# Casting all weight pieces before the next x, and multiplying before transposing, in a batched matmul on one core

## The chip, the cores and the metric

The kernel runs on one core of one Trainium2 chip. The metric is the time of one execution on the device, in microseconds; a smaller time is better. Each of the core's engines runs its own queue of instructions in order: TensorE (PE) multiplies and transposes, VectorE (DVE) and ScalarE (ACT) copy and convert, SyncE (SP) issues the transfers, GpSimd (POOL) only builds an identity matrix at the start. They wait for one another through counting semaphores. Sixteen transfer (DMA) engines move data between the device's memory (HBM) and the on-chip buffers.

## The reference

128 independent products of a 256x512 matrix with a 512x384 matrix, all in float32:

```python
b1, b2, m, k, n = 8, 16, 256, 512, 384
x = randn(b1, b2, m, k); weight = randn(b1, b2, k, n)
out = np.matmul(x, weight)
```

## The kernel before

**Groups.** Four batch items form a group (`G = 4`), so there are `NG = 32` groups, numbered 0 to 31. For each group SP loads x (2048 KB) and the weights (3072 KB) as float32 and stores the result (1536 KB). x and weights have two buffers each in float32 (`XS`, `WS`), the results four (`OS`).

**What each engine does for a group.**

- VectorE converts x to bf16 in four pieces (`cast_x`, line 171; one piece is two of a partition's eight rows). There is one bf16 buffer for x (`BS = 1`), so piece q of a group waits until TensorE has transposed piece q of the group before (`t_made`).
- The weights are converted to bf16 in sixteen pieces of 32 partitions x 1536 elements (`cast_w`, line 184): the first `CV` by VectorE, the last `CA` by ScalarE, with `CV + CA = 16`. Before the change these are 11 and 5. The bf16 weights have room for two groups (`WBS = 2 * G`), so casting a group waits for the multiplication of the group before the last (`p_made`). In groups 0 to 3, 30 and 31 (`is_short`) VectorE converts all weights in eight pieces of 64 partitions (`cast_short`, line 200) and ScalarE only counts its semaphore up.
- TensorE transposes x in four quarters of four instructions each (`transpose`, line 224) into PSUM (`pt`, four buffers); ScalarE copies each quarter to the on-chip buffer `x_t` (`evacuate`, line 211).
- TensorE multiplies in four quarters of 32 instructions (`multiply`, line 242), each on a 32-column strip of the array; the last group has another layout (`multiply_full`, line 260). A multiplication first waits for all sixteen weight pieces of its group (`w_acast`, `w_vcast`), then, quarter by quarter, for the copied transposes (`t_copied`) and for a free result buffer (`o_copied`; `po` has two).
- ScalarE copies each quarter's result out of PSUM (`copy_out`, line 275).

**The order on SP** (`on_sync`). For each group m from 4 on: load x of m (after `x_cast` of group m-2), store the result of group m-4 (after its `copy_out`), load the weights of m (after both engines' casts of group m-2). Each of these waits holds up what is behind it on SP.

**The order on VectorE** (`on_vector`, `step`). For group n: eight weight pieces (`XV = 8`), then the four pieces of x of group n+1, then the other three weight pieces of n.

**The order on TensorE** (`on_tensor`). Transposes of group n+1, then the multiplication of group n; the loop handles two groups per turn.

**The order on ScalarE** (`on_scalar`, `step`). For group n: copy three quarters of the transposes of n+1, copy out the first quarter of n, copy the last quarter of the transposes, then copy out the other quarters of n; after the second and the third copy-out one weight piece each of group n+1, and after the fourth the remaining three.

Of the kernel before, what the change touches and what calls it, by code (L numbers as in the profile page):

```python
# [12 lines left out]
def kernel(  # L13
# [30 lines left out]
    T = R // 2  # L44
# [6 lines left out]

    LAG = 4

    CA = 5
    CV = G * SL - CA
    HV = G * SH

    XV = 8

    PAD = 12  # L60

# [58 lines left out]
    def is_short(n):  # L120
        return isinstance(n, int) and (n < LAG or n >= NG - 2)
# [4 lines left out]
    def load_w(e, t, U, s):  # L126
        n = t * U + s
        if not isinstance(n, int) or n >= WS:
            e.wait_ge(w_vcast, n * CV + (1 - WS) * CV)
            e.wait_ge(w_acast, n * CA + (1 - WS) * CA)  # L130
        d = SL // SH if is_short(n) else 1
# [32 lines left out]
    def cast_x(e, t, U, s, q):  # L164
        n = t * U + s
        if q == 0:
            e.wait_ge(x_in[s % XS], (t * (U // XS) + s // XS) * 16 + 16)
        e.wait_ge(t_made, n * T + (q + 1 - T + BIAS))  # L168
        rows = slice(2 * q, 2 * q + 2)
        S = SH if is_short(n) else SL  # L170
        e.tensor_copy(  # L171
            out=x_bf[s % BS][:, rows].rearrange("p r (s q c) -> p r s q c", s=S, c=KO),
            in_=x_sb[s % XS][:, rows].rearrange("p r (q s c) -> p r s q c", s=S, c=KO),
        ).then_inc(x_cast, 1)

    def cast_w(e, t, U, s, parts, first=True):
        n = t * U + s
        if first:
            e.wait_ge(p_made, n * T + (BIAS - T))
            e.wait_ge(w_in[s % WS], (t * (U // WS) + (s - LAG) // WS) * 16 + 16)  # L180
        copy = e.tensor_copy if e is nc.vector else e.copy
        for c in parts:
            i, h = c // SL, c % SL
            copy(  # L184
                out=w_bf[(s * G + i) % WBS][h * C : (h + 1) * C],
                in_=w_sb[s % WS][i * C : (i + 1) * C, h * KO : (h + 1) * KO, :],
            ).then_inc(w_vcast if c < CV else w_acast, 1)

    def cast_short(e, n):
        e.wait_ge(p_made, n * T + (BIAS - T))  # L190
        p = P // SH
        for d in range(SL // SH):
            turns = n // WS if n < LAG else LAG // WS
            e.wait_ge(h_in[n % WS * 2 + d], turns * 16 + 16)  # L194
            for a in range(SH):
                for h in range(SH):
                    c = d * 4 + a * 2 + h
                    r = (d * SH + h) * KO

                    e.tensor_copy(  # L200
                        out=w_bf[(n * G + d * SH + a) % WBS][h * p : (h + 1) * p],
                        in_=w_sb[n % WS][a * p : (a + 1) * p, r : r + KO, :],
                    ).then_inc(w_vcast, 2 if c < CV - HV else 1)

    def evacuate(e, t, U, s, parts=range(T)):
        n = t * U + s
        if parts[0] == 0:
            e.wait_ge(p_made, n * T + (BIAS - T))
        for q in parts:
            e.wait_ge(t_made, n * T + (q + 1 + BIAS))  # L210
            e.copy(  # L211
                out=x_t[s % TS][:, 2 * q : 2 * q + 2],
                in_=pt[(s * T + q) % PT][:].bitcast(bf16),
            ).then_inc(t_copied, 1)

    def transpose(e, t, U, s):
        n = t * U + s
        words = x_bf[s % BS][:].bitcast(fp32)
        for q in range(T):
            e.wait_ge(x_cast, n * T + (q + 1))  # L220
            e.wait_ge(t_copied, n * T + (q + 1 - PT + BIAS))
            for rr in range(2):
                for h in range(KO // 2):
                    ins = e.transpose(  # L224
                        pt[(s * T + q) % PT][:, rr, h, :],
                        words[:, 2 * q + rr, h :: KO // 2],
                        identity[:],
                    )
            ins.then_inc(t_made, 1)

    def multiply(e, t, U, s):
        n = t * U + s
        e.wait_ge(w_acast, n * CA + CA)
        e.wait_ge(w_vcast, n * CV + CV)
        for q in range(T):
            e.wait_ge(t_copied, n * T + (q + 1 + BIAS))
            e.wait_ge(o_copied, n * T + (q + 1 - PO + BIAS))
            for rr in range(2):
                for ko in range(KO):
                    for i in range(G):  # L240
                        mine = slice(i * C, (i + 1) * C)
                        ins = e.matmul(  # L242
                            po[(s * T + q) % PO][mine, rr, :N],
                            x_t[s % TS][:, 2 * q + rr, ko // 2, mine, ko % 2],
                            w_bf[(s * G + i) % WBS][:, ko, :],
                            start=(ko == 0),
                            stop=(ko == KO - 1),
                        )
            ins.then_inc(p_made, 1)

    def multiply_full(e, t, U, s):
        n = t * U + s
        e.wait_ge(w_acast, n * CA + CA)
        e.wait_ge(w_vcast, n * CV + CV)
# [14 lines left out]
    def copy_out(e, t, U, s, q):  # L269
        n = t * U + s  # L270
        if q == 0:
            if not isinstance(n, int) or n >= OS:
                e.wait_ge(o_out[s % 2], (t * (U // 2) + s // 2) * 16 + (16 - OS // 2 * 16 + 16))
        e.wait_ge(p_made, n * T + (q + 1 + BIAS))
        e.copy(  # L275
            out=out_sb[:, bass.ds(slot(t, U, s) * R + 2 * q, 2), :],
            in_=po[(s * T + q) % PO][:, :, :N],
        ).then_inc(o_copied, 1)
# [33 lines left out]
    def on_vector(e):  # L312
        U = 2

        def next_x(t, U, s):
            for q in range(T):
                cast_x(e, t, U, s + 1, q)

        def step(t, U, s):
            n = t * U + s  # L320
            if is_short(n):
                cast_short(e, n)
            else:
                cast_w(e, t, U, s, range(XV))
            if not isinstance(n, int) or n < NG - 1:
                next_x(t, U, s)
            if not is_short(n):
                cast_w(e, t, U, s, range(XV, CV), False)

        next_x(0, NG, -1)  # L330
        for n in range(LAG):
            step(0, NG, n)
        rounds = (NG - 3 - LAG) // U
        with e.Fori(0, rounds) as t:  # L334
            for s in range(U):
                step(t, U, LAG + s)
        for n in range(LAG + rounds * U, NG):
            step(0, NG, n)

    def on_tensor(e):  # L340
        U = 2
        e.sem_inc(t_made, BIAS)
        e.sem_inc(p_made, BIAS)
        e.wait_ge(id_done, 2)
        transpose(e, 0, NG, 0)

        pe = mybir.EngineType.PE
        with nc.Fori(0, NG // U, engines=OrderedEngineSet([pe]), head_slot={pe: 0}) as t:
            transpose(e, t, U, 1)
            multiply(e, t, U, 0)  # L350
            with e.If(t < NG // U - 1):
                transpose(e, t, U, 2)
                multiply(e, t, U, 1)
            with e.Else():
                multiply_full(e, t, U, 1)

    def on_scalar(e):
        U = 2
        e.sem_inc(t_copied, BIAS)
        e.sem_inc(o_copied, BIAS)  # L360
        for s in range(2):
            e.sem_inc(o_out[s], 16)

        def step(t, U, s):
            short = is_short(t * U + s + 1)
            evacuate(e, t, U, s + 1, range(T - 1))
            for q in range(T):
                copy_out(e, t, U, s, q)  # L370
                if q == 0:
                    evacuate(e, t, U, s + 1, range(T - 1, T))
                if q == 0 and short:
                    e.sem_inc(w_acast, CA)
                if q > 0 and not short:
                    last = CA if q == T - 1 else q
                    cast_w(e, t, U, s + 1, range(CV + q - 1, CV + last), q == 1)

        evacuate(e, 0, NG, 0)
        e.sem_inc(w_acast, CA)  # L380
        for n in range(LAG - 1):
            step(0, NG, n)
        rounds = (NG - 2 - LAG) // U
        with e.Fori(0, rounds) as t:
            for s in range(LAG - 1, LAG - 1 + U):
                step(t, U, s)
        for n in range(LAG - 1 + rounds * U, NG - 1):
            step(0, NG, n)
        for q in range(T):
            copy_out(e, 0, NG, NG - 1, q)  # L390

    on_gpsimd(nc.gpsimd)
    on_sync(nc.sync)
    on_vector(nc.vector)
    on_tensor(nc.tensor)
    on_scalar(nc.scalar)

# [29 lines left out]
```

## Time and profile before

| | |
|---|---|
| time, median of 3 runs (lowest to highest) | 517.62 us (517.43 to 517.68) |
| profiled execution | 517.57 us, its span 515.8 us |
| TensorE: matmul busy, mean granted clock | 320.0 us (62%), 0.778 of full |
| VectorE busy | 397.7 us (77%) |
| ScalarE busy | 409.7 us (79%) |
| transfers' share of the 16 engines' span | 99.3%, 218.11 MB, mean 423 GB/s |
| VectorE weight cast, 32x1536 (line 184) | x286, mean 951 ns |
| ScalarE weight cast, 32x1536 (line 184) | x130, mean 1470 ns |
| VectorE x cast (line 171) | x128, mean 688 ns |
| ScalarE copy of transposes (line 211) | x128, mean 1021 ns |
| ScalarE copy-out (line 275) | x128, mean 800 ns |
| 3072 KB of weights, issue to landing (median) | 18.2 us |
| 2048 KB of x, issue to landing (median) | 22.3 us |
| 1536 KB of result, issue to landing (median) | 25.0 us |

The span runs from the first to the last instruction of the profiled execution. Busy times are sums of instruction durations; where instructions overlap in an engine's pipeline, the distance from one start to the next can be shorter than a duration. The times to landing contain the time that a transfer stands behind others. The granted clock is the share of its full speed that TensorE's clock has at a time.

### The profile page before, as it was taken

What the parts mean: (1) busy time and instruction counts of PE and PEld (TensorE: products, weight loads), DVE (VectorE), ACT (ScalarE), POOL (GpSimd) and SP (SyncE); (2) the same over time, 40 slices, a digit from 0 to 9 for tenths busy, and PEclk for the clock granted to TensorE, in tenths of its full rate; (3) what the DMA queues carried; (4) which work ended last, traced back from release to release, by engine and by line L of the source; (5) the groups of instructions that cost most, each with busy time, mean ns of one, the idle gap of its engine ahead of it and who ended that gap; (6) DMA issues with size and microseconds to landing.
All of it is one profiled execution on the core that took longest, in us unless ns stands there. A gap on an engine that the chain in (4) does not pass through costs nothing.

```text
span 515.8 us, 11659 instructions
## 1 busy us (share of the span) xinstructions
PE 320.0 (62%) x4512; PEld 222.0 (43%) x4512; DVE 397.7 (77%) x462; ACT 409.7 (79%) x387; POOL 0.7 (0%) x6
## 2 busy tenths in 40 slices
PE   2276737567586656675655864767657477656871
PEld 2254425444354443453443543535445354434550
DVE  2788757788777897777977778877789777797960
ACT  1365577798978997987998799889798978997751
POOL 0000000000000000000000000000000000000000
PEclk9698878677866877876888686778667876877697
DMA  8999999999999999999999999999999999999996
GB/s 337 428 423 426 437 430 420 435 431 433 431 424 432 430 439 428 429 426 432 433 436 428 423 434 431 437 429 425 430 431 434 433 429 427 430 435 423 421 429 250
DMA packets 15462, 218.18 MB, mean 423 GB/s; under 512 B 1632, under 2 KB 1632, under 8 KB 2656
## 3 DMA queue, kind: packets, MB, share of 16 engines
q1 hardware_dynamic: 15456, 218.11, 99.3%
q8 instruction: 3, 0.05, 0.0%
q14 instruction: 3, 0.02, 0.0%
HBM read 167.77 MB, written 50.33 MB: 423 GB/s over the span
## 4 chain that ended last, share of the span: by engine, by line
DMA 57%; DVE 29%; issue 9%; PE 1%; DVEq 1%; SPq 1%; ACT 0%; POOLq 0%
DMA w_sb<-in_weight_dram 57%; DVE w_bf L184 20%; DVE x_bf L171 5%; DVE w_bf L200 4%; PE po L260 1%; SPq L135 0%; DVEq L334 0%; SPq L118 0%; DVEq L62 0%; DVEq L180 0%; ACT out_sb L275 0%; SPq L130 0%; DVEq L168 0%; DVEq L194 0%; SPq L422 0%
## 5 line engine op out<-in xcount | busy, mean ns | idle before, releaser
L184 DVE CAST w_bf<-w_sb 32x1536 bf16<-32x1536 f32 x286 | 271.9, 951 | 81.1 <-DMA w_sb<-in_weight_dram 73.0
L242 PE MATMUL po<-w_bf,x_t 128*32 128x384 bf16 x3968 | 201.5, 364 | 33.4 <-DVE w_bf L184 25.4
L224 PE MATMUL pt<-identity,x_bf 128*128 128x128 f32 x512 | 113.5, 409 | 149.1 <-DVE x_bf L171 149.1
L184 ACT CAST w_bf<-w_sb 32x1536 bf16<-32x1536 f32 x130 | 191.0, 1470 | 5.1 <-DMA w_sb<-in_weight_dram 1.9
L224 PEld LDWEIGHTS pt<-identity,x_bf 128*128 128x128 f32 x512 | 101.3, 223 | 161.5 <-issue 161.0
L242 PEld LDWEIGHTS po<-w_bf,x_t 128*32 128x32 bf16 x3968 | 117.7, 107 | 116.3 <-issue 51.5
L275 ACT COPY out_sb<-po 128x768 f32 (+1 forms) x128 | 102.5, 800 | 59.7 <-PE po L242 53.9
L211 ACT COPY x_t<-pt 128x1024 bf16<-128x1024 bf16 x128 | 123.6, 1021 | 20.9 <-PE pt L224 20.3
L171 DVE CAST x_bf<-x_sb 128x1024 bf16<-128x1024 f32 x128 | 80.0, 688 | 12.5 <-DMA x_sb<-in_x_dram 11.7
L200 DVE CAST w_bf<-w_sb 64x1536 bf16<-64x1536 f32 x48 | 45.8, 955 | 8.3 <-DMA w_sb<-in_weight_dram 7.0
L211 ACT ACT_TABLE_LOAD x1 | 1.3, 1283 | 10.8 <-PE pt L224 10.8
L260 PE MATMUL po<-w_bf,x_t 128*128 128x384 bf16 x32 | 5.4, 326 | 2.8 <-DVE w_bf L200 2.8
L260 PEld LDWEIGHTS po<-w_bf,x_t 128*128 128x128 bf16 x32 | 3.1, 98 | 5.1 <-issue 3.1
masks.py:199 POOL TENSOR_SCALAR_AFFINE_SELECT identity<-identity 128x128 f32<-128x128 f32 x1 | 0.3, 294 | 0.2 <-POOL identity L281 0.2
L281 POOL MEMSET identity<- 128x128 f32 x1 | 0.2, 205 | 0.5 <-POOLq L62 0.5
L411 POOL MEMSET const-bfloat16-1.0<- 128x1 bf16 x1 | 0.1, 102 | 0.0
L411 POOL MEMSET const-uint8-127<- 128x1 uint8 x1 | 0.1, 102 | 0.0
L411 POOL MEMSET const-float32-0.0<- 128x1 f32 x1 | 0.1, 99 | 0.2 <-issue 0.2
L411 POOL MEMSET const-float32-1.0<- 128x1 f32 x1 | 0.1, 99 | 0.0
## 6 DMA issues: line engine op xcount, KB each, us to landing
w_sb<-in_weight_dram SPq DMA_DIRECT2D x26, 3072.0 KB, 18.2
x_sb<-in_x_dram SPq DMA_DIRECT2D x32, 2048.0 KB, 22.3
out_dram<-out_sb SPq DMA_DIRECT2D x32, 1536.0 KB, 25.0
w_sb<-in_weight_dram SPq DMA_DIRECT2D x12, 1536.0 KB, 16.7
```

What stands on the lines that cost most here:

```text
L171: e.tensor_copy(out=x_bf[s % BS][:, rows].rearrange("p r (s q c) -> p r s q c", s=S, c=KO), in_=x_sb[s % XS][:, rows].rearrange("p r (q s ...
L184: copy(out=w_bf[(s * G + i) % WBS][h * C : (h + 1) * C], in_=w_sb[s % WS][i * C : (i + 1) * C, h * KO : (h + 1) * KO, :],).then_inc(w_vcas ...
L200: e.tensor_copy(out=w_bf[(n * G + d * SH + a) % WBS][h * p : (h + 1) * p], in_=w_sb[n % WS][a * p : (a + 1) * p, r : r + KO, :],).then_inc ...
L211: e.copy(out=x_t[s % TS][:, 2 * q : 2 * q + 2], in_=pt[(s * T + q) % PT][:].bitcast(bf16),).then_inc(t_copied, 1)
L224: ins = e.transpose(pt[(s * T + q) % PT][:, rr, h, :], words[:, 2 * q + rr, h :: KO // 2], identity[:],)
L242: ins = e.matmul(po[(s * T + q) % PO][mine, rr, :N], x_t[s % TS][:, 2 * q + rr, ko // 2, mine, ko % 2], w_bf[(s * G + i) % WBS][:, ko, :], ...
L260: ins = e.matmul(po[(s * T + q) % PO][:, rr, :N], x_t[s % TS][:, 2 * q + rr, ko // 2, :, ko % 2], w_bf[(s * G + q) % WBS][:, ko, :], start ...
L275: e.copy(out=out_sb[:, bass.ds(slot(t, U, s) * R + 2 * q, 2), :], in_=po[(s * T + q) % PO][:, :, :N],).then_inc(o_copied, 1)
L281: e.memset(identity[:], 0.0).then_inc(id_done, 1)
L411: nc = _bacc.Bacc("TRN2", target_bir_lowering=False, num_devices=1)
```

## The change

Three orders change together. VectorE casts twelve weight pieces instead of eleven, all in a row, and only then the next x (`XV` is gone). ScalarE casts four instead of five, and its order becomes: copy out quarters 0, 1 and 2 of group n; one weight piece of n+1; copy out quarter 3; a second weight piece; copy all four quarters of the transposes of n+1; the last two weight pieces. TensorE multiplies group n and only then transposes group n+1; the transposes of group 0 still stand ahead of the loop.

```diff
-    CA = 5
+    CA = 4
     CV = G * SL - CA
     HV = G * SH
-
-    XV = 8
...
-                cast_w(e, t, U, s, range(XV))
+                cast_w(e, t, U, s, range(CV))
             if not isinstance(n, int) or n < NG - 1:
                 next_x(t, U, s)
-            if not is_short(n):
-                cast_w(e, t, U, s, range(XV, CV), False)
...
+            multiply(e, t, U, 0)
             transpose(e, t, U, 1)
-            multiply(e, t, U, 0)
             with e.If(t < NG // U - 1):
+                multiply(e, t, U, 1)
                 transpose(e, t, U, 2)
-                multiply(e, t, U, 1)
             with e.Else():
                 multiply_full(e, t, U, 1)
...
             short = is_short(t * U + s + 1)
-            evacuate(e, t, U, s + 1, range(T - 1))
             for q in range(T):
                 copy_out(e, t, U, s, q)
-                if q == 0:
-                    evacuate(e, t, U, s + 1, range(T - 1, T))
                 if q == 0 and short:
                     e.sem_inc(w_acast, CA)
-                if q > 0 and not short:
-                    last = CA if q == T - 1 else q
-                    cast_w(e, t, U, s + 1, range(CV + q - 1, CV + last), q == 1)
+                if q == T - 2 and not short:
+                    cast_w(e, t, U, s + 1, range(CV, CV + 1))
+            if not short:
+                cast_w(e, t, U, s + 1, range(CV + 1, CV + 2), False)
+            evacuate(e, t, U, s + 1)
+            if not short:
+                cast_w(e, t, U, s + 1, range(CV + 2, CV + CA), False)
```

## The prediction, made before the changed kernel ran

> M(n) is the multiplication of group n, T(n) its transposes; c is how long M(n) runs at half clock before the full clock is granted.
>
> **What bounds the kernel now.** I read the page's slices and its chain first, then the waits, then the timeline of all engines in the middle, then the granted clock in short stretches.
>
> ```profile
> DMA  8999999999999999999999999999999999999996
> GB/s 337 428 423 426 437 430 420 435 431 433 431 424 432 430 439 428 429 426 432 433 436 428 423 434 431 437 429 425 430 431 434 433 429 427 430 435 423 421 429 250
> DMA 57%; DVE 29%; issue 9%; PE 1%; DVEq 1%; SPq 1%; ACT 0%; POOLq 0%
> ```
>
> The transfer engines never pause. A group moves 2048 + 3072 + 1536 KB = 6.82 MB, at 430 GB/s 15.9 us; M(5) starts at 99.36 and M(29) at 480.53, so 381.17/24 = 15.88 us a group. Transfers set the period, and 73 us of DVE's idle time wait for weights. Engine work has cover as long as a group's round stays under 15.88 us.
>
> In the timeline (start, us, engine, line, operation; idle before in brackets) one group reads:
>
> ```profile
> 244.47 7.83 DVE L184 CAST w_bf<-w_sb 32x1536 bf16<-32x1536 f32 x8 [2.59 <-DMA w_sb<-in_weight_dram]
> ...
> 249.24 0.80 ACT L275 COPY out_sb<-po 128x768 f32 x1
> 250.07 1.47 ACT L184 CAST w_bf<-w_sb 32x1536 bf16<-32x1536 f32 x1
> 251.44 0.78 ACT L275 COPY out_sb<-po 128x768 f32 x1
> 252.25 4.46 ACT L184 CAST w_bf<-w_sb 32x1536 bf16<-32x1536 f32 x3
> 252.34 2.50 DVE L171 CAST x_bf<-x_sb 128x1024 bf16<-128x1024 f32 x4
> 253.16 3.25 PEld L224 LDWEIGHTS pt<-identity,x_bf 128*128 128x128 f32 x16 [4.18 <-issue]
> 253.16 3.44 PE L224 MATMUL pt<-identity,x_bf 128*128 128x128 f32 x16 [3.79 <-DVE x_bf L171]
> 254.87 2.91 DVE L184 CAST w_bf<-w_sb 32x1536 bf16<-32x1536 f32 x3
> 256.73 2.85 ACT L211 COPY x_t<-pt 128x1024 bf16<-128x1024 bf16 x3
> 257.99 2.42 PEld L242 LDWEIGHTS po<-w_bf,x_t 128*32 128x32 bf16 x64 [1.58 <-ACT x_t L211]
> 258.02 5.80 PE L242 MATMUL po<-w_bf,x_t 128*32 128x384 bf16 x128 [1.42 <-DVE w_bf L184]
> ```
>
> DVE's last weight cast (ends 257.78) releases M(n). ScalarE's five casts ended at 256.71, and it copies the transposes out before and under M(n): nothing of ScalarE lies between two multiplications. The last quantity I need is M's speed:
>
> ```profile
> 480.53 7.51 PE L242 MATMUL po<-w_bf,x_t 128*32 128x384 bf16 x128 [1.17 <-DVE w_bf L184]
> ...
> 483.38 0.80 ACT L275 COPY out_sb<-po 128x768 f32<-128x768 f32 x1 [1.43 <-PE po L242]
> ...
> 485.49 0.80 ACT L275 COPY out_sb<-po 128x768 f32<-128x768 f32 x1 [0.40 <-PE po L242]
> 486.79 0.80 ACT L275 COPY out_sb<-po 128x768 f32<-128x768 f32 x1 [0.50 <-PE po L242]
> ```
>
> A copy starts when a quarter of M is done: the first 2.85 us after M's start, the third after 6.26; at full clock quarters are 1.30 apart. The granted clock in half-microsecond stretches says when it is full:
>
> ```profile
> 245.50:246.00 0.50, 0.50 (x13) 0.24 (x8) 0.50 (x1) 0.50 (x2) 0.00 (x0) 0.53 1.08 459
> 256.00:256.50 0.50, 0.50 (x4) 0.41 (x3) 0.50 (x1) 0.50 (x1) 0.00 (x0) 0.79 0.91 393
> 273.00:273.50 0.50, 0.00 (x0) 0.00 (x0) 0.50 (x1) 0.50 (x2) 0.00 (x0) 0.72 0.96 410
> 293.50:294.00 0.50, 0.50 (x16) 0.32 (x12) 0.47 (x2) 0.50 (x1) 0.00 (x0) 0.74 0.96 410
> ```
>
> (The third number from the end is the clock.) A stretch whose mean is 0.79 was at 0.5 for the first 42% of it and at 1 for the rest. So full clock came at 245.97, 256.21, 273.28 and 293.76. The gaps are 10.24, 17.07 and 20.48: 3, 5 and 6 times 3.41. Here the clock is raised only on a fixed grid of 3.41 us. On that grid (67 steps after 256.21) the switch in the M of 480.53 falls at 484.9, so c was 4.37 there.
>
> **The change, part by part.**
>
> *DVE:* twelve weight casts in a row, then x. Eight take 7.83, so one step is 0.983 and twelve take 11.76, after the weights have landed. Before it was 7.83 + 2.53 + 2.94 = 13.3. DVE's round is 11.76 + 2.5 + gaps = 14.4, under the period: 1.5 us earlier with the weights, nothing on the path once ScalarE is later. The x casts come later by 3.9, but T(n+1) now waits behind M(n) anyway, which starts after DVE's twelve; cost nothing, cover about 4 us. SP issues load x (n+3) only behind load w (n+2), which waits for ScalarE's last cast; by then x (n+1) is cast, except at the first long group, where SP waits 2.3 us with over 15 us of queue in front of the transfers (weights take 18.2 us from issue to landing): nothing.
>
> *TensorE:* M(n), then T(n+1). M no longer follows transposes but an idle stretch, and starts at half clock: every T after an idle gap of 3.29 us or more took 3.33 to 3.69 us, the one after a gap of 1.00 took 2.54.
>
> *ScalarE*, the path. M(n+1) waits for the four casts of group n+1, and the last two stand behind all copies of the transposes, which stand behind the last copy-out of M(n). From the start of the third copy-out of M(n), start to start by the rows above: copy to cast 0.83, cast to copy 1.37, copy to cast 0.81, cast to copy of transposes 1.49 (4.46/3), three steps of 0.91 ((2.85-1.02)/2) and one of 1.04 to the next cast, then 1.49 + 1.47, and 0.03 to M (305.41 to 305.44, where a copy of ScalarE released it). Sum 11.26. T(n+1) does not delay it: M(n) ends 7.1 after its start (7.51 less 0.44 for the shorter c found below) and the first quarter of T(n+1) is there at about 8.1, while ScalarE asks at 10.3. The weights don't either: in the first such round they land at 85.82 and ScalarE asks at about 88.7.
>
> The third copy starts 6.26 after M's start with c = 4.37; a microsecond at half clock delays by 0.5. So **the round is 6.26 + 11.26 + 0.5(c - 4.37) = 15.33 + 0.5c.**
>
> *What c is* has no row, since no M before followed a long idle stretch. T(n+1) ends 9.7 after M(n) starts, so PE idles some 7 us. Both ends from the grid: TensorE was busy in 66% of the step from 239.14 to 242.56 and got no full clock; 79% of the step from 269.87 to 273.28 was enough. So c is at least 0.66 x 3.41 = 2.3 and at most 0.79 x 3.41 + 3.41 = 6.1; rounds from 16.5 to 18.4, all above 15.88. Between the ends I take the value at which the round repeats itself: if a round exceeds five grid steps (17.07), the next M starts that much later against the grid and its c is shorter by as much. c' = c - (15.33 + 0.5c - 17.07) settles by halves at c = 3.5, whatever the start, and a small error of my 15.33 only moves c. The round is then **17.07 us**.
>
> Would a lower price do? The Trainium skill (TensorE: Matmul & The Clock Gate, Part 1: The HAM clock gate) says that for modelling the ramp costs under 1% of a typical kernel's span. By it the sum would be at most 517.6 + 5.2 = 522.8. This trace agrees so far (M's of 7.51 beside 5.80 cost nothing), but here transfers hide them, and after the change nothing would.
>
> **Sum.** The first long group's weights land at 69.94 as before (start-up is transfers). M(4) starts at 69.94 + 11.76 + 0.24 = 81.94 (was 83.47; ScalarE is ready at 80.5). M(29) follows 25 rounds later: 81.94 + 426.75 = 508.7, within 2 us for settling. Then M(29) 7.1 and T(30) 2.54, DVE's x casts of group 31 chasing it to about 10.6, eight weight casts 7.86, 0.23: the last M starts 18.7 after M(29). From there to the end of the span 15.9 as before (499.91 to 515.8). The weights of 31, issued at M(29) into a short queue, need 7.3 at 430 GB/s and about 2 to start (the share is 0.56 in the span's first 4 us), so they land before 10.6; four stores of 3.7 then end at about 24.5, before the last is issued at 24.9. Span 508.7 + 34.6 = 543.3. The profiled execution took 517.57 for a span of 515.8, so 1.77 lies around it; the median of the runs is 517.62, the same. **545.1 us.**
>
> **Rivals.**
> - *No settling:* c wanders between its ends, mean 4.2, round 17.43, 25 x 0.36 more: 554; with c at 6.1 always 578. For it: other periods may jitter the start. Against: ScalarE's steps repeat to 0.02 us. 0.14.
> - *Short cold stretches:* c near 2.3 to 2.7, round 16.5 to 16.7: 530 to 535. Needs M to start always at the same early place of a grid step, which the round itself moves. 0.08.
> - *The other side, M at full clock:* if c is under (15.88 - 15.33)/0.5 = 1.1 us, ScalarE's round is under the period, transfers stay the bound, M(4)'s earlier start is lost in the queue or kept: 517.6 down to 515.5. For it: the clock stays full 2.5 to 4 us after an M ends. Against: PE idles 7. The page's 1% rule belongs here, and would give up to 522.8. 0.05.
> - That the order isn't what the diff says is excluded: the counts of both casting engines add up to sixteen and M waits for all.
>
> **How the numbers follow.** Forecast 0.73, rivals 0.14, 0.08, 0.05. Range 533 to 562: the forecast's own is 541 to 549; the low end takes in part of the short stretches, the high end most of the unsettled cases, which leaves out about 1 in 7. About 0.2% (1 us) can be told from no change; the full-clock case is split between faster (0.025) and same (0.025), all else is slower (0.95).
>
> **What would show it.** M starts 17.07 apart, each at clock 0.5 for about 3.5 us; M released by ScalarE's weight cast; chain mostly ScalarE and PE; transfers' share near 515.8/543 of before, about 94%, and weights landing some 10 us after issue, not 18.2. DVE waits for PE rather than DMA before x casts. Wrong if M starts stay 15.9 apart, or M is released by DVE.

## The result and the profile after

The changed kernel takes 543.52 us (median of 6 runs, 542.25 to 545.46), the kernel before 517.65 us (6 runs, 517.38 to 517.97). The ratio is 1.050, 95% interval 1.048 to 1.052: slower by 25.9 us. The profiled execution of the changed kernel took 543.83 us, its span is 542.0 us.

From the page of the changed kernel: the transfers' rate in forty slices, the chain that ended last by engine and by line, and the share of the transfer queue (lines have moved: 182 is the weight cast, 209 the copy of transposes, 222 the transposes, 240 the multiplication, 273 the copy-out).

```profile
GB/s 342 428 427 425 432 430 425 431 424 435 433 427 435 414 398 407 403 394 398 390 413 405 394 387 392 422 398 385 396 391 420 398 382 401 391 427 397 303 385 317
...
q1 hardware_dynamic: 15456, 218.11, 98.8%
...
ACT 28%; DMA 27%; PE 23%; issue 11%; DVE 8%; ACTq 1%; SPq 0%; DVEq 0%; POOLq 0%
DMA w_sb<-in_weight_dram 27%; PE po L240 22%; ACT w_bf L182 17%; ACT x_t L209 10%; DVE w_bf L198 4%; DVE w_bf L182 4%; ACT out_sb L273 1%; PE po L258 1%; DVE x_bf L169 0%; ACTq L208 0%; PE pt L222 0%; SPq L133 0%; ACTq L273 0%; DVEq L60 0%; ACTq L381 0%
```

The chain was transfers and VectorE; it is now half ScalarE and TensorE. The transfers' rate falls from some 430 GB/s to about 400 after the first third. The queue's share alone would have hidden that: it is 98.8%, where it was 99.3%.

One round in the timeline of the changed kernel (start, us, engine, line, operation; in brackets the idle time before it and who ended it):

```profile
270.92 6.77 PE L240 MATMUL po<-w_bf,x_t 128*32 128x384 bf16 x128 [8.19 <-ACT w_bf L182]
...
276.54 0.81 ACT L273 COPY out_sb<-po 128x768 f32 x1 [0.49 <-PE po L240]
277.23 1.47 ACT L182 CAST w_bf<-w_sb 32x1536 bf16<-32x1536 f32 x1
...
277.62 2.18 PE L222 MATMUL pt<-identity,x_bf 128*128 128x128 f32 x16
278.61 0.78 ACT L273 COPY out_sb<-po 128x768 f32 x1
...
279.42 1.47 ACT L182 CAST w_bf<-w_sb 32x1536 bf16<-32x1536 f32 x1
280.91 3.76 ACT L209 COPY x_t<-pt 128x1024 bf16<-128x1024 bf16 x4
284.69 2.96 ACT L182 CAST w_bf<-w_sb 32x1536 bf16<-32x1536 f32 x2
...
287.98 6.78 PE L240 MATMUL po<-w_bf,x_t 128*32 128x384 bf16 x128 [8.17 <-ACT w_bf L182]
```

From the third copy-out at 276.54 ScalarE works without a gap until 287.65, and 0.33 us later the next multiplication starts. TensorE is idle for 8.2 us before it. The third copy-out starts 5.62 us after the multiplication does. Together 17.06 us, where the period before was 15.88. The two multiplications take 6.77 and 6.78 us, longer than the 5.80 of a full-clock one before.

The granted clock is the third number from the end of a stretch:

```profile
290.50:291.00 0.50, 0.50 (x12) 0.29 (x8) 0.50 (x1) 0.02 (x1) 0.00 (x0) 0.65 1.11 467
...
307.50:308.00 0.50, 0.50 (x12) 0.30 (x8) 0.47 (x2) 0.00 (x0) 0.00 (x0) 0.58 1.34 565
...
324.50:325.00 0.50, 0.50 (x16) 0.21 (x8) 0.50 (x1) 0.00 (x0) 0.00 (x0) 0.52 1.32 541
```

Read as in the prediction, full clock comes at 290.85, 307.92 and 324.98, that is 2.87, 2.86 and 2.87 us after the multiplications of 287.98, 305.06 and 322.11. The rounds are 17.08 and 17.05. The clock's grid and the rounds run in step. The first rounds of the same kernel show how they got there:

```profile
81.85 7.43 PE L240 MATMUL po<-w_bf,x_t 128*32 128x384 bf16 x128 [14.10 <-DVE w_bf L182]
...
99.58 7.10 PE L240 MATMUL po<-w_bf,x_t 128*32 128x384 bf16 x128 [8.19 <-ACT w_bf L182]
...
116.97 6.94 PE L240 MATMUL po<-w_bf,x_t 128*32 128x384 bf16 x128 [8.17 <-ACT w_bf L182]
...
134.22 6.85 PE L240 MATMUL po<-w_bf,x_t 128*32 128x384 bf16 x128 [8.19 <-ACT w_bf L182]
```

These are groups 4 to 7. Rounds of 17.73, 17.39 and 17.25 exceed 17.07 by 0.66, 0.32 and 0.18: the excess about halves each time.

**Where the 26.2 us of span went.** From M(4) to M(29), 25 rounds: 428.0 us (81.85 to 509.86) against 397.1 (83.47 to 480.53), 30.9 more. M(4) starts 1.6 earlier. From M(29) to the end of the span 32.1 against 35.3, 3.1 less. 30.9 - 1.6 - 3.1 = 26.2.

### The profile page after: what moved, and what is told of

The parts are those of the page before. It is cut to its first block, busy times and chain, and to the rows that moved or that the text cites. A ratio compares the mean times of both kernels' runs of the same rounds, so it can differ in the third digit from the quotient of the medians.

```text
span 542.0 us, 11643 instructions
## 1 busy us (share of the span) xinstructions
PE 286.7 (53%) x4512; PEld 190.8 (35%) x4512; DVE 422.3 (78%) x488; ACT 370.6 (68%) x361; POOL 0.7 (0%) x6
## 3 DMA queue, kind: packets, MB, share of 16 engines
q1 hardware_dynamic: 15456, 218.11, 98.8%
## 4 chain that ended last, share of the span: by engine, by line
ACT 28%; DMA 27%; PE 23%; issue 11%; DVE 8%; ACTq 1%; SPq 0%; DVEq 0%; POOLq 0%
DMA w_sb<-in_weight_dram 27%; PE po L240 22%; ACT w_bf L182 17%; ACT x_t L209 10%; DVE w_bf L198 4%; DVE w_bf L182 4%; ACT out_sb L273 1%; PE po L258 1%; DVE x_bf L169 0%; ACTq L208 0%; PE pt L222 0%; SPq L133 0%; ACTq L273 0%; DVEq L60 0%; ACTq L381 0%
## 5 line engine op out<-in xcount | busy, mean ns | idle before, releaser
L182 DVE CAST w_bf<-w_sb 32x1536 bf16<-32x1536 f32 x312 | 296.7, 951 | 80.7 <-DMA w_sb<-in_weight_dram 71.8
L240 PE MATMUL po<-w_bf,x_t 128*32 128x384 bf16 x3968 | 212.2, 384 | 236.0 <-ACT w_bf L182 139.1
L240 PEld LDWEIGHTS po<-w_bf,x_t 128*32 128x32 bf16 x3968 | 122.6, 112 | 319.5 <-issue 263.5
L182 ACT CAST w_bf<-w_sb 32x1536 bf16<-32x1536 f32 x104 | 152.6, 1467 | 6.5 <-DMA w_sb<-in_weight_dram 4.6
L209 ACT COPY x_t<-pt 128x1024 bf16<-128x1024 bf16 x128 | 120.3, 1027 | 0.7
L222 PE MATMUL pt<-identity,x_bf 128*128 128x128 f32 x512 | 71.4, 293 | 9.6 <-DVE x_bf L169 9.6
L222 PEld LDWEIGHTS pt<-identity,x_bf 128*128 128x128 f32 x512 | 65.1, 209 | 19.4 <-issue 19.4
## 6 DMA issues: line engine op xcount, KB each, us to landing
w_sb<-in_weight_dram SPq DMA_DIRECT2D x26, 3072.0 KB, 15.6
```

The source lines that it names most:

```text
L182: copy(out=w_bf[(s * G + i) % WBS][h * C : (h + 1) * C], in_=w_sb[s % WS][i * C : (i + 1) * C, h * KO : (h + 1) * KO, :],).then_inc(w_vcas ...
L209: e.copy(out=x_t[s % TS][:, 2 * q : 2 * q + 2], in_=pt[(s * T + q) % PT][:].bitcast(bf16),).then_inc(t_copied, 1)
L222: ins = e.transpose(pt[(s * T + q) % PT][:, rr, h, :], words[:, 2 * q + rr, h :: KO // 2], identity[:],)
L240: ins = e.matmul(po[(s * T + q) % PO][mine, rr, :N], x_t[s % TS][:, 2 * q + rr, ko // 2, mine, ko % 2], w_bf[(s * G + i) % WBS][:, ko, :], ...
```

## The experiments

Three questions are asked: is it ScalarE's two casts behind the copies of the transposes; is it the half clock; and does the round really settle on the grid, or is 17.07 a sum that happens to fall there? All times are medians beside runs of the kernel before on the same chip (517.57 or 517.71 us). Diffs are against the changed kernel unless said.

### All of ScalarE's casts ahead of the copies of the transposes: 517.81 us

```diff
-                cast_w(e, t, U, s + 1, range(CV + 1, CV + 2), False)
+                cast_w(e, t, U, s + 1, range(CV + 1, CV + CA), False)
             evacuate(e, t, U, s + 1)
-            if not short:
-                cast_w(e, t, U, s + 1, range(CV + 2, CV + CA), False)
```

> ScalarE casts all four of its weight pieces before it copies the transposes; VectorE's and TensorE's new orders stay. Theory (ScalarE's two casts behind the copies of the transposes close the round): the next multiplication then waits only for the first copied quarter, so the round is 12.6 us plus half of the half-clock time c, at most 15.65 with c = 6.1, under the 15.88 us of the transfers. Time 515.5 to 519 us, multiplications some 15.9 us apart. Rival (multiplying before transposing, at half clock, is dear in itself, or VectorE's late x is): the time stays above 530 us.

Ratio to before 1.000 (0.9995 to 1.0014): the whole loss is gone with two casts moved, while VectorE's twelve in a row and TensorE's new order stay. Two multiplications from its timeline:

```profile
288.58 7.28 PE L240 MATMUL po<-w_bf,x_t 128*32 128x384 bf16 x128 [7.14 <-ACT x_t L209]
...
304.41 7.89 PE L240 MATMUL po<-w_bf,x_t 128*32 128x384 bf16 x128 [6.43 <-DVE w_bf L182]
```

They start at half clock too (7.28 and 7.89 us long), 15.83 us apart. The first row names a copy of the transposes as what ended the wait, but VectorE's last weight cast ended 0.2 us ahead of each of the two (at 288.34 and 304.18): the multiplication waits for VectorE's casts again, and these for the transfers, which move 430 GB/s between 240 and 480 us as before the change. A slow multiplication costs nothing as long as the round ends under the transfers' period. The half clock alone does not make the loss.

### Three casts ahead, one behind: 544.92 us

```diff
-                cast_w(e, t, U, s + 1, range(CV + 1, CV + 2), False)
+                cast_w(e, t, U, s + 1, range(CV + 1, CV + 3), False)
             evacuate(e, t, U, s + 1)
             if not short:
-                cast_w(e, t, U, s + 1, range(CV + 2, CV + CA), False)
+                cast_w(e, t, U, s + 1, range(CV + 3, CV + CA), False)
```

> The changed kernel with three of ScalarE's four weight pieces ahead of the copies of the transposes and one behind. Theory (what counts is whether the last piece stands behind the copies, since then all of ScalarE's work lies between two multiplications): the sum of the round is the same, multiplications 17.07 us apart, 542 to 545 us. Rival (each piece behind the copies costs its own 1.47 us): half of the loss is gone, about 530 us.

Ratio 1.052 (1.050 to 1.055), the loss unchanged. Two multiplications:

```profile
270.44 6.77 PE L240 MATMUL po<-w_bf,x_t 128*32 128x384 bf16 x128 [8.19 <-DVE w_bf L182]
...
287.49 6.78 PE L240 MATMUL po<-w_bf,x_t 128*32 128x384 bf16 x128 [8.16 <-DVE w_bf L182]
```

They stay 17.05 to 17.08 us apart. The time alone would not tell the theory from the rival, since a round that settles can hide 1.47 us (two experiments on, it does). What tells is that the multiplications still take the changed kernel's 6.77 us, so that c has not grown, and that from the third copy-out (276.06) to the next multiplication it is still 11.43 us, beside 11.44. A piece behind the copies has no price of its own: with one there, the multiplication still waits until ScalarE has done everything.

### TensorE kept busy: 545.00 us with 48 idle transposes, 520.05 us with 64

```diff
+    def filler(e, t, U, s):
+        n = t * U + s
+        e.wait_ge(o_copied, n * T + (1 - PO + BIAS))
+        for _ in range(FILL):
+            e.transpose(po[(s * T) % PO][:, 0, :P], identity[:], identity[:])
...
             transpose(e, t, U, 1)
             with e.If(t < NG // U - 1):
+                filler(e, t, U, 1)
                 multiply(e, t, U, 1)
                 transpose(e, t, U, 2)
+                with e.If(t < NG // U - 2):
+                    filler(e, t, U, 2)
```

> The changed kernel with 48 more transposes of the identity, into a free result buffer, between the transposes of a group and its multiplication (groups 1 to 29), so that TensorE is not idle there. Theory (the half-clock start is what lifts the round over the transfers' period): multiplications run at full clock, the round without c is 15.6 us, under 15.88, time 516 to 521 us. Rival (the order of ScalarE alone makes the loss, whatever the clock): about 543 us.

With 48 the time did not move (1.052, 1.050 to 1.054), against the theory as expected. The timeline and the clock of that run say why:

```profile
281.31 5.40 PE L235 MATMUL po<-identity 128*128 128x128 f32 x48
...
289.64 6.78 PE L248 MATMUL po<-w_bf,x_t 128*32 128x384 bf16 x128 [2.92 <-ACT w_bf L182]
```

```profile
288.50:289.00 0.50, 0.00 (x0) 0.00 (x0) 0.47 (x2) 0.50 (x1) 0.00 (x0) 1.00 1.17 426
289.00:289.50 0.50, 0.00 (x0) 0.00 (x0) 0.50 (x1) 0.31 (x1) 0.00 (x0) 0.60 0.95 385
289.64:292.00 2.36, 2.36 (x32) 1.27 (x36) 2.27 (x4) 0.00 (x0) 0.00 (x0) 0.50 1.03 403
```

The filler ended at 286.71, 2.9 us too early, and the clock dropped at 289.10, half a microsecond before the multiplication. So the next run has 64:

> As the run with 48 transposes of the identity, with 64. With 48 TensorE was idle for only 2.96 us before each multiplication, and the clock still dropped just ahead of it (at 289.3, the multiplication at 289.64). Theory: 64 leave a gap of about 1.2 us, the clock stays full through it, the round without c is 15.6 us and the transfers' 15.88 decide, time 516 to 521 us. Rival (the clock is not what lifts the round): again about 544 us.

```profile
280.12 7.15 PE L235 MATMUL po<-identity 128*128 128x128 f32 x64
288.83 5.48 PE L248 MATMUL po<-w_bf,x_t 128*32 128x384 bf16 x128 [1.56 <-DVE w_bf L182]
```

The gap is 1.56 us, the multiplication takes 5.48 us at full clock (a granted clock of 1.00 between 240 and 480 us, where the changed kernel has 0.80), VectorE releases it again, and 23.5 of the 25.9 us are back (ratio to before 1.005, 1.003 to 1.006). Of the 2.3 us of span that are left over the kernel before, 0.6 have come by M(29) (481.15, where it was 480.53) and the rest in the last two groups. ScalarE's order is the changed kernel's, unaltered. So the half clock is necessary for the loss, and extra work on TensorE makes the kernel faster because it keeps the clock up. Slower transfers are not the cause: their 399 GB/s between 240 and 480 us in the changed kernel are 430 again here, with the same loads and stores.

### Half a piece and a whole piece off ScalarE: 544.75 and 543.83 us

In the first, VectorE casts half the columns of ScalarE's last piece:

```diff
-    CV = G * SL - CA
+    CV = 13
+    AV = 12
+    HALF = 15
...
-            cast_w(e, t, U, s, range(CV))
+            cast_w(e, t, U, s, [*range(AV), HALF], half=(KO // 2, KO))
...
-                cast_w(e, t, U, s + 1, range(CV + 2, CV + CA), False)
+                cast_w(e, t, U, s + 1, range(AV + 2, AV + CA), False, half=(0, KO // 2))
```

> The changed kernel with half a weight piece moved from ScalarE to VectorE, 0.64 us less on ScalarE's part of the round. Theory (the round settles at five steps of the clock's grid): multiplications still 17.07 us apart, each 1.3 us longer at half clock (c 2.9 to about 4.2), time 541 to 543.5 us. Rival (the round is a plain sum with c as it is): 25 rounds of 0.64 us less, about 527.5 us.

In the second, a whole piece moves:

```diff
-    CA = 4
+    CA = 3
```

> The changed kernel with thirteen weight pieces on VectorE and three on ScalarE, 1.47 us less on ScalarE's part of the round. Theory (settling): five grid steps ask for c = 5.8, at the upper end of what is possible (5.7 to 6.1). Either the rounds stay at 17.07 with multiplications half-clocked for 5.8 us and the time is 540 to 543 us, or c falls back by a step now and then, rounds are unequal with a mean of about 16.6 and the time is 527 to 537 us. Rival (plain sum with c = 2.9): round 15.6, so the transfers' 15.88, 517 to 519 us.

Neither is faster (ratios 1.052, 1.050 to 1.054, and 1.049, 1.047 to 1.051; the plain sums gave 527.5 and 517 to 519). Both lie above the theory's ranges, by 1.3 and 0.8 us, though the rounds are as forecast. A multiplication of the first run, then three of the second:

```profile
288.06 7.42 PE L243 MATMUL po<-w_bf,x_t 128*32 128x384 bf16 x128 [7.52 <-DVE w_bf L185]
```

```profile
287.40 7.99 PE L240 MATMUL po<-w_bf,x_t 128*32 128x384 bf16 x128 [6.95 <-ACT w_bf L182]
304.47 7.99 PE L240 MATMUL po<-w_bf,x_t 128*32 128x384 bf16 x128 [6.96 <-ACT w_bf L182]
321.52 8.00 PE L240 MATMUL po<-w_bf,x_t 128*32 128x384 bf16 x128 [6.95 <-DVE w_bf L182]
```

The second run's are 17.07 and 17.05 apart, as in the changed kernel, though a piece of 1.47 us is gone from ScalarE: from the third copy-out (294.24) to the next multiplication it is 10.23 us, where it was 11.44. The multiplications have stretched from 6.77 to 7.42 and 8.0 us. Read from the clock as above (a mean of 0.82 between 275.0 and 275.5 us in the first run, where a multiplication started at 271.01, and of 0.69 between 309.5 and 310.0 in the second), full clock comes 4.17 us after the start with half a piece less and 5.34 with a piece less, where it was 2.87. What ScalarE saves, the clock takes.

### Half a piece more on ScalarE: 584.74 us

```diff
-    CA = 4
-    CV = G * SL - CA
+    CA = 5
+    CV = 12
+    HALF = 11
...
-            cast_w(e, t, U, s, range(CV))
+            cast_w(e, t, U, s, range(CV), half=(0, KO // 2))
...
-                cast_w(e, t, U, s + 1, range(CV + 2, CV + CA), False)
+                cast_w(e, t, U, s + 1, [CV + 2, CV + 3, HALF], False, half=(KO // 2, KO))
```

> The changed kernel with half a weight piece moved from VectorE to ScalarE, 0.64 us or a little more on ScalarE's part of the round. Theory (settling): the c that five steps would ask for, 1.6 us, lies below the shortest possible of about 2.3, so the rounds can't settle at 17.07; c jumps up by a step and falls again, rounds are unequal, between 17.4 and 19, mean about 18.0, time 562 to 574 us. Rival (plain sum): equal rounds of 17.7 us, about 559.5 us.

Ratio 1.130 (1.128 to 1.132): more than either theory gave. Multiplications in the middle:

```profile
269.19 6.94 PE L242 MATMUL po<-w_bf,x_t 128*32 128x384 bf16 x128 [9.16 <-ACT w_bf L184]
287.44 8.04 PE L242 MATMUL po<-w_bf,x_t 128*32 128x384 bf16 x128 [9.20 <-DVE w_bf L184]
306.75 6.93 PE L242 MATMUL po<-w_bf,x_t 128*32 128x384 bf16 x128 [9.16 <-ACT w_bf L184]
324.97 8.05 PE L242 MATMUL po<-w_bf,x_t 128*32 128x384 bf16 x128 [9.17 <-DVE w_bf L184]
```

Rounds of 18.25 and 19.31 alternate. Two of them are 37.56, eleven steps of 3.414: the rounds do run in step with the grid, but only every second one falls on it. After a round of 18.25 with c = 3.2 the next c would be 3.2 - (18.25 - 17.07) = 2.0, which is too short to get the clock, so it is 2.0 + 3.4 = 5.4 (measured 5.43; TensorE was busy in 59% of the step that ended 2.0 us after the start of 287.44, and the clock stayed at 0.50); after 19.31 it is 5.43 - 2.24 = 3.2 again. My number failed twice: from the third copy-out (274.98) to the next multiplication it is 12.46 us, 1.0 more than in the changed kernel and not 0.64 (the last casts take 3.81 instead of 2.96, and the step from the third copy-out to the cast 0.83 instead of 0.69), and I averaged over c instead of following the pairs. A plain sum with 1.0 would give 543.5 + 25 x 1.0 = 568.5 us.

### VectorE's order alone, against the kernel before: 522.40 us

```diff
-    CA = 5
+    CA = 4
-    XV = 8
+    XV = CV
...
-            if not is_short(n):
-                cast_w(e, t, U, s, range(XV, CV), False)
```

> The kernel before with twelve weight pieces in a row on VectorE before the next x, and four on ScalarE behind the second, third and fourth copy-outs; TensorE still transposes before it multiplies and ScalarE copies the transposes first. Theory (VectorE's order has cover): transfers stay the bound, 516.5 to 519 us, the multiplication starting some 2 us later after its weights land. Rival (later x casts cost on their own): 1 us or more per group, over 540 us.

Ratio 1.009 (1.0075 to 1.0108): both numbers miss, the theory's by 3.4 us. From its timeline:

```profile
273.55 2.50 DVE L171 CAST x_bf<-x_sb 128x1024 bf16<-128x1024 f32 x4
...
274.38 3.69 PE L224 MATMUL pt<-identity,x_bf 128*128 128x128 f32 x16 [6.86 <-DVE x_bf L171]
...
278.00 6.02 PE L242 MATMUL po<-w_bf,x_t 128*32 128x384 bf16 x128
```

With transposes ahead of the multiplication, the late x casts stand in the multiplication's way: it starts 4.45 us after the first x cast does, and no longer right behind the last weight cast. Between 120 and 480 us the transfers run at 429 to 431 GB/s as in the kernel before, so the period is the same there; but each multiplication starts later in its round, M(29) at 486.75 where it was 480.53, and at the end this shows: the last group's multiplication starts at 504.58, where it was 499.91, and the span is 4.6 us longer. In the changed kernel the multiplication stands first, and this cost does not arise: with ScalarE's casts moved ahead it is back to 517.8.

No run beat the kernel before.

## Why the prediction was right

- *The round of ScalarE bounds the kernel: right.* From the third copy-out to the next multiplication 11.44 us were measured, 11.26 predicted. The way from ScalarE's cast to TensorE took 0.33 us, where I had taken 0.03 from a copy of transposes that was probably not what released that multiplication (VectorE's last weight cast had ended at 305.16, 0.28 us before it). The step from the third copy-out to the cast was shorter, 0.69 instead of 0.83, which gives back about half.
- *M starts at half clock, and c settles where the round is five grid steps: right,* 17.07 as predicted, with c = 2.87 instead of 3.5. The longer sum and the shorter c are one thing: the third copy-out came 0.1 us later than the prediction gives for this c, the rest of the round was 0.2 longer, and the settling made c 0.6 shorter to make up for these 0.3, as the prediction said it would. There was some luck in it: c can't be much under 2.3, so a sum longer by another 0.3 us (an estimate, half of 2.87 less 2.3) would have left no c to settle at, and the run with half a piece more shows what comes then, rounds of 18.8 us on average. The two runs with less work on ScalarE and the pairs of the run with more confirm the settling beyond one value; a plain sum misses all three.
- *c lies between 2.3 and 6.1:* where it was read, it was between 2.86 and 5.43, and a needed 2.0 was not reached.
- *VectorE's order costs nothing: right for this kernel*, by 517.81 with it; not right by itself, by 522.40. The reason given, that the transposes wait behind M(n) anyway, holds only together with TensorE's order.
- *M(4) at 81.94, M(29) at 508.7:* 81.85 and 509.86. The rounds on the way to settling added 1.2 us, inside the 2 that were allowed.
- *The end, 34.6 us from M(29):* mis-sized, 32.1. The last multiplication started 18.1 after M(29) (predicted 18.7), and from there the span ended 14.1 us later, not 15.9 as before. The last store took less time (issued when the last copy-out ended at about 534.1, 7.9 us before the end; before it was 9.7). Why, no run shows. This error and the 1.2 us of the line above have opposite signs, and together they make the predicted span 1.3 us too long, 543.3 beside 542.0.
- *What would show it:* multiplications 17.07 apart, half-clocked, released by ScalarE's cast (139 us of TensorE's waiting is put down to that, 79.5 to VectorE's casts; 14.1 of these are M(4), which did wait for VectorE, but in the settled rounds VectorE had ended long before, for the multiplication of 305.06 at 296.99): right. *Transfers' share 94% and weights landing 10 us after issue: wrong.* The share is 98.8% and the weights land after 15.6 us. The rate shows what I meant: 399 GB/s between 240 and 480 us at a share of 1.00, where the kernel of the first experiment moves 430 at the same share. The Trainium skill (Perfetto Trace Analysis, Identifying the Most-Contended Engine) says to judge transfers by HBM utilization and not by occupancy, which sixteen engines make misleading; this trace agrees, with rates of 399 and 430 GB/s at the same share. *VectorE waiting for TensorE ahead of its x casts: wrong*, it waits for weights (71.8 us) since they land later than I took.
- *The half clock costs more than 1% of the span: right.* With the clock held up by 64 transposes a group the changed kernel is 23.5 us faster, 4.3% of 543.5. The Trainium skill (TensorE: Matmul & The Clock Gate, Part 1: The HAM clock gate) says that for modelling the ramp costs under 1% of a typical kernel's span; not so here, where each round starts at half clock and no transfer hides it.

## What to carry to other kernels

Where a loop's round passes through TensorE after an idle stretch, take the half-clock time from the clock's grid and ask whether the round, including it, still fits under the bound; if it doesn't, the round can settle on a multiple of the grid step, and small savings or costs elsewhere in it then change nothing, or far more than their size. Look at what the last wait of a multiplication has queued ahead of it on the releasing engine: here a single weight cast behind the four copies, together with the half clock, was enough for the whole loss. When a saving on the path brings nothing, look at whether another term grew by as much before calling it off the path.

## What was not expected of the hardware

- A gap of 2.9 us on TensorE was enough to lose the full clock just ahead of the next multiplication (the step of the grid that ended at 289.10 was busy for its first 1.0 us only); a gap of 1.6 us was not.
- The transfers' share of time says little about spare room: 1.00 at 399 GB/s and 1.00 at 430. Why the packets take longer when less is moved was not tried.
- Sixty-four float32 transposes a group, 7.15 us of useless work, made the changed kernel 23.5 us faster.
